# Modulation blocks in bursts of eight and four, with borrowed weight buffers, on one Trainium2 core

## The chip, the core and the metric

The kernel runs on one core of one Trainium2 chip. The time is device microseconds (us) of one execution; three runs of the kernel before gave a median of 3060.91 us. TensorE (PE) multiplies, VectorE (DVE) and ScalarE (ACT) work on its results, SyncE (SP) issues the weight transfers.

## The reference

One layer of a decoder, float32 throughout, for 256 prompt tokens and 8 sequences of 4 sample tokens (T = 288 columns), D = 4096:

```
mod = silu(c) @ w_ada + b_ada  -> shift, scale, gate        # 9 rows of c, w_ada 4096 x 12288
h   = x * (1 + scale) + shift                               # 288 x 4096
[q|k|v|z_a|u|v_b|z_b|g_a|g_b] = h @ w_in                    # 4096 x 18944
A = sliding_window_attention(q, k, v, sinks) * silu(z_a)
B = u * (W_s @ LN(v_b) + b_s) * silu(z_b)
m = sigmoid(g_a) * (A @ w_pa) + sigmoid(g_b) * (B @ w_pb)
x = LayerNorm(ALPHA * x + gate * (m @ w_o))
```

`h` needs all of c's products for its own columns, so the first matmul with `w_in` has to wait for a part of `mod`.

## The kernel before

**Layout.** Features lie on partitions, tokens on the free axis: a *column tile* is 128 output features x 288 tokens, a *k tile* (kt) 128 of the 4096 input features (32 of them). Each weight is read once, in units of 128 x 2048 numbers (1 MB), each by one transfer of SP into a tile `raw` (five buffers, `RAW`). Where the unit is for a main product, ACT rounds it to `wH` (float32r) and DVE takes the rest `wL = raw - wH`, 128 x 1024 at a time (lines 182 and 183). A product of one 128 x 128 block is then three matmuls with 288 columns, `wH*xH`, `wH*xL`, `wL*xH` (`prod`, lines 194 to 196). Sums stand in three PSUM buffers (`acc`); DVE or ACT takes each finished one out.

**Modulation.** The shift and scale columns of w_ada are cut into *chunks* of k tiles, `CHUNKS = [1, 2, 2, 2, 1, 4, 4, 8, 8]`; a chunk of n has 4n blocks of 1 MB (`ada_units`). These are not split: a block is 4 float32 matmuls with 32 stationary columns and 512 moving ones (8 of 256 or 16 of 128 in small chunks), line 234, in four column strips of the array. In the trace each of them stands as two records, in the program as one. After a chunk's last block `fin` lets DVE copy the sums out (`adae`), and a background generator `modulate` has PE transpose them (`adaT`) and DVE and ACT form, k tile by k tile, `xs = x*scale + shift`, `hH` and `hL` (lines 286 to 299).

**Early units.** 56 of the 148 column tiles of `w_in` (part of g_a, k, v, q) are computed chunk by chunk as `h` grows: 113 units in all, `early_units`, tile `ea`. For each column tile and chunk, `early_post` adds the PSUM sum to an accumulator in SBUF (`Q`, `accA`, `accB`, `xs`, lines 340 to 356). A unit of a chunk of n has 16/n column tiles, so 3n matmuls lie between two such sums. The rest of `w_in` (`rest_units`, tile `in`) runs later with 16 k tiles per sum; of 32 of these (zb and u) the half that needs only the first 16 k tiles may run earlier (`extra`).

**What sets the order.** `first_order` writes the order of modulation blocks and early units by a running credit: in the first half (16 k tiles) blocks and early units alternate at a ratio of 1.6 in groups of about two, in the second half two blocks and two other units. It keeps two early units of a chunk (one of the first) back until the next chunk's blocks are through. `run` issues each unit's transfer and split two units ahead. `pump`, called before each product, runs background generators against a credit of 100 for each product; `ensure_h` runs them at once if a unit needs an `h` not yet made. The tile framework then orders instructions within each engine, and each engine executes its own in that order. SP's transfers wait for a free `raw` and for one of eight semaphores that they share with ACT's.

Eight large SBUF buffers (`slot`, 128 x 4608) hold in this stage xs, hH0, hH1, hL0, hL1 (the rounded `h` and its rest, 16 k tiles each), Q, accA and accB.

Of the kernel before, what the change touches and what calls it, by code (L numbers as in the profile page):

```python
# [10 lines left out]
F32 = mybir.dt.float32  # L11
F32R = mybir.dt.float32r
# [6 lines left out]
P = 128  # L19
# [13 lines left out]
TB = 96  # L33
UNIT = 2048

CHUNKS = [1, 2, 2, 2, 1, 4, 4, 8, 8]
RAW = 5
HB = 3
RES = 2
RES0 = 1  # L40
HSTEP = 1
RATIO2 = 1.0
XT = tuple('zb,u'.split(','))
RATIO = 1.6
GE2 = 2.0
GE = 2.0
CAP = 1.5

OFFS = [sum(CHUNKS[:i]) for i in range(len(CHUNKS))]
CQ, CK, CV, CZA, CU, CVB, CZB, CGA, CGB = 0, 16, 18, 20, 36, 52, 68, 84, 116  # L50
# [24 lines left out]
def first_order(au, eu, extra):  # L75

    order = []
    ada = [(c, u) for c, us in enumerate(au) for u in us]  # L80
    early = [(c, u) for c, us in enumerate(eu) for u in us]
    extra = list(extra)
    credit, at, go = 0.0, -1, False
    half = OFFS.index(KT // 2)
    while ada:
        at = ada[0][0]
        ratio = RATIO if at < half else RATIO2
        ready = early and early[0][0] < at
        if ready and at < half and early[0][0] == at - 1 and sum(1 for x in early if x[0] == at - 1) <= (RES if at > 1 else RES0):
            ready = False  # L90
        if credit < 1.0:
            go = False
        elif credit >= (GE if at < half else GE2):
            go = True
        if go and ready:
            order.append(early.pop(0)[1])
            credit -= 1.0
        elif go and at >= half and extra:
            order.append(extra.pop(0))
            credit -= 1.0  # L100
        else:
            order.append(ada.pop(0)[1])
            credit = min(credit + 1.0 / ratio, CAP + 1.0 / ratio + (GE if at < half else GE2) - 1.0)
    return order, extra[:4] + [u for _, u in early] + extra[4:]


def bc(ap, axis, shape):
    return ap.unsqueeze(axis).to_broadcast(list(shape))


def build(ctx, tc, nc, I, O):
    sb = lambda name, bufs=1: ctx.enter_context(tc.tile_pool(name=name, bufs=bufs))
    const, slots, wp, tmp = sb("const"), sb("slots", 8), sb("wp", 4), sb("tmp", 2)
# [6 lines left out]
    def slot(name, shape=(P, 16, T), dt=F32):  # L120
        return slots.tile(list(shape), dt, tag="s", name=name)
# [4 lines left out]
    def bgp(name):  # L126
        return ps_bg.tile([P, 512], F32, tag="bg", name=name)
# [12 lines left out]
    nc.scalar.dma_start(lngb, I["lngb"])  # L140
    nc.vector.memset(epst, EPS)

    hH = [slot(f"hH{i}", dt=F32R) for i in range(2)]
    hL = [slot(f"hL{i}", dt=F32R) for i in range(2)]
    pdram = dram.tile([len(REST), P, T], F32, name="pdram")
    gdram = dram.tile([64, P, T], F32, name="gdram")

# [3 lines left out]
    credit = [0.0]  # L151
# [15 lines left out]
    class Unit:  # L167
        def __init__(self, src, body, split=True, blocks=16):
            self.src, self.body, self.split, self.blocks = src, body, split, blocks

        def start(self):
            raw = wp.tile([P, UNIT], F32, tag="raw", name="raw", bufs=RAW)
            w = self.blocks * P
            nc.sync.dma_start(raw[:, :w], self.src[:, :w])
            self.raw = raw
            self.H, self.L = [], []
            if self.split:
                for hf in range(w // 1024):
                    s = raw[:, hf * 1024:(hf + 1) * 1024]
                    h = wp.tile([P, 1024], F32R, tag="wH", name="wH", bufs=HB)  # L180
                    lo = wp.tile([P, 1024], F32R, tag="wL", name="wL", bufs=HB)
                    nc.scalar.copy(h, s)  # L182
                    nc.vector.tensor_sub(lo, s, h.bitcast(F32))  # L183
                    self.H.append(h)
                    self.L.append(lo)
# [60 lines left out]
    def ada_copies(ps, w):  # L246
        out = []
        for a in range(0, w, 256):
            e = tmp.tile([P, T], F32, tag="t", name="adae", bufs=6)
            nc.vector.tensor_copy(e[:, :min(w - a, 256)], ps[:, a:min(w, a + 256)])  # L250
            out += [e[:, b:b + P] for b in range(0, min(w - a, 256), P)]
        return out

    def ada_transposed(blocks):
        tp = bgp("adaT")
        for i, e in enumerate(blocks):
            nc.tensor.transpose(tp[:, i * P:(i + 1) * P], e, ident)
        return tp[:, :len(blocks) * P].rearrange("p (tb q b) -> p q tb b", q=4, b=32)
# [9 lines left out]
    def load_x(c):  # L268
        n, o = CHUNKS[c], OFFS[c]
        nc.scalar.dma_start(xs[:, 0, :n], I["xT"][:, o:o + n])  # L270

    def ada_fin(c):
        n, o = CHUNKS[c], OFFS[c]

        def modulate(blocks):
            mod = tmp.tile([P, 2, 8, 9], F32, tag="mod", name="mod", bufs=2)
            tpv = ada_transposed(blocks)
            if n < 8:
                b1 = bada[:, :64].rearrange("p (s k) -> p s k", s=2)[:, :, o:o + n]
                nc.vector.tensor_tensor(mod[:, :, :n], tpv[:, 0:2, :, 0:9], bc(b1, 3, (P, 2, n, 9)), ALU.add)  # L280
                nc.vector.tensor_tensor(mod[:, :, :n], mod[:, :, :n], tpv[:, 2:4, :, 0:9], ALU.add)
            else:
                for s in range(2):
                    out = mod[:, s].rearrange("p (q tb) b -> p q tb b", q=2)
                    b1 = bada[:, 32 * s + o:32 * s + o + n].rearrange("p (q tb) -> p q tb", q=2)
                    nc.vector.tensor_tensor(out, tpv[:, 2 * s:2 * s + 2, :, 0:9], bc(b1, 3, (P, 2, 4, 9)), ALU.add)
            nc.vector.tensor_scalar_add(mod[:, 1, :n], mod[:, 1, :n], 1.0)
            for k in range(0, n, HSTEP):
                w = min(HSTEP, n - k)
                x = xs[:, 0, k:k + w]  # L290
                for i in range(w):
                    nc.vector.tensor_scalar(x[:, i, :NPR], x[:, i, :NPR], mod[:, 1, k + i, 0:1], mod[:, 0, k + i, 0:1],
                                            ALU.mult, ALU.add)
                xv = x[:, :, NPR:].rearrange("p n (b t) -> p n b t", t=TS)
                nc.vector.tensor_tensor(xv, xv, bc(mod[:, 1, k:k + w, 1:9], 3, (P, w, NB, TS)), ALU.mult)
                nc.vector.tensor_tensor(xv, xv, bc(mod[:, 0, k:k + w, 1:9], 3, (P, w, NB, TS)), ALU.add)
                a, b = (o + k) // 16, (o + k) % 16
                nc.scalar.copy(hH[a][:, b:b + w], x)  # L298
                nc.vector.tensor_sub(hL[a][:, b:b + w], x, hH[a][:, b:b + w].bitcast(F32))  # L299
            if c + 1 < len(CHUNKS):  # L300
                load_x(c + 1)
            h_done.add(c)
            yield 300

        def fin(ps):
            bg.insert(0, modulate(ada_copies(ps, P * n if n < 8 else 512)))
        return fin

    def gate_fin(gc):
        def finish(blocks):  # L310
            tpv = ada_transposed(blocks)
            out = gate[:, 16 * gc:16 * gc + 16].rearrange("p (q tb) b -> p q tb b", q=4)
            b1 = bada[:, 64 + 16 * gc:80 + 16 * gc].rearrange("p (q tb) -> p q tb", q=4)
            nc.vector.tensor_tensor(out, tpv[:, :, :, 0:9], bc(b1, 3, (P, 4, 4, 9)), ALU.add)
            yield 300

        def fin(ps):
            bg.insert(0, finish(ada_copies(ps, 512)))
        return fin
# [16 lines left out]
    def early_post(e, ps, c):  # L336
        ct, d = EARLY[e], early_dst(e)
        if c == 0:
            if e % 2:
                nc.scalar.copy(d, ps)  # L340
            else:
                nc.vector.tensor_copy(d, ps)
        elif c < len(CHUNKS) - 1:
            nc.vector.tensor_add(d, d, ps)
# [21 lines left out]
    def early_units(c):  # L366
        n, o = CHUNKS[c], OFFS[c]
        per = 16 // n
# [532 lines left out]
    items = []  # L901
# [17 lines left out]
    au = [ada_units(n, ada_fin(c)) for c, n in enumerate(CHUNKS)]  # L919
    gu = [u for gc in range(GATE_CHUNKS) for u in ada_units(8, gate_fin(gc))]  # L920
    eu = [early_units(c) for c in range(len(CHUNKS))]
    extra = [ru[r][0] for r, (k, _) in enumerate(REST) if k in XT]
    order, rest = first_order(au, eu, extra)
    items += order
    ru = [us[1:] if k in XT else us for us, (k, _) in zip(ru, REST)]
    n_vb = sum(k == "vb" for k, _ in REST)
    body = rest + flat(ru[:first_vb]) + [drain] + flat(ru[first_vb:first_vb + 2 * n_vb]) + [drain]
# [4 lines left out]
    order = [pu[0][0], pu[1][0], pu[0][1]]  # L932
# [96 lines left out]
```

## Time and profile before

| what | value |
|---|---|
| runs | 3060.25, 3060.91, 3063.03 us |
| the profiled execution | 3059.19 us, of which the span of the program is 3057.4 us |
| PE busy | 3017.8 us of the span |
| DVE, ACT busy | 1571.4 us, 1077.9 us |
| PE idle before 24 us / from 24 to 600 us / from 600 to 1000 us | 15.5 / 12.7 / 0 us |
| bytes read from memory | 676.85 MB |

Modulation and early units fill the stretch from 0 to about 823 us of the span. In the profile, times stand in us from the start of the span; `[2.00 <-ACT wH L182]` behind a row is idle time of that engine before it, and what ended it. A PE that is busy all the time can still be slow: a matmul is shown for some 0.29 us while the next starts 0.13 us after it, so what counts is the step from one start to the next.

### The profile page before, as it was taken

How to read it: one execution, taken by the hardware profiler on the slowest of the kernel's cores; microseconds unless marked ns; L12 is line 12 of the kernel's file. 1: busy time of each engine (PE TensorE's matmuls, PEld its weight loads, DVE VectorE, ACT ScalarE, POOL GpSimd, SP SyncE). 2: the span in 40 equal slices, each digit the busy share in tenths (PEclk: the TensorE clock that was granted, in tenths of full speed). 3: DMA queues.
4: the chain of work that ended last, by engine and by line, in shares of the span. 5: the costliest groups of instructions: out<-in, count | busy, mean ns of one | idle time of the engine just before them, and what ended most of it. 6: DMA issues, size and time to landing. Idle time of an engine off the chain costs nothing.

```text
span 3057.4 us, 53584 instructions
## 1 busy us (share of the span) xinstructions
PE 3017.8 (99%) x23168; PEld 2844.2 (93%) x23168; DVE 1571.4 (51%) x2262; ACT 1077.9 (35%) x1381; POOL 17.5 (1%) x16
## 2 busy tenths in 40 slices
PE   7999999999999999999999999999999999999998
PEld 6887888888999999999999999999999999999997
DVE  4777554444445545454444643445555555555555
ACT  3222322322332434344333333333444444433333
POOL 0000000000000000000000000000000000000001
PEclk9999999999999999999999999999999999999998
DMA  8888877877767565565655565666565555555552
GB/s 328 334 321 323 340 281 285 318 262 286 276 235 249 198 221 211 209 219 191 217 193 207 207 216 215 222 226 222 196 218 187 187 188 189 175 177 177 177 177 96
DMA packets 128672, 700.09 MB, mean 229 GB/s; under 512 B 14834, under 2 KB 44818, under 8 KB 49298
## 3 DMA queue, kind: packets, MB, share of 16 engines
q1 hardware_dynamic: 109584, 669.56, 60.6%
q10 hardware_dynamic: 18852, 27.10, 2.5%
q8 instruction: 182, 2.98, 0.4%
q14 instruction: 54, 0.44, 0.0%
HBM read 676.85 MB, written 19.46 MB: 228 GB/s over the span
## 4 chain that ended last, share of the span: by engine, by line
PE 97%; DVE 1%; DMA 1%; issue 0%; ACT 0%; DVEq 0%; SPq 0%; ACTq 0%
PE in L194 13%; PE in L196 13%; PE in L195 13%; PE ea L194 8%; PE ea L196 8%; PE ea L195 8%; PE ada L234 5%; PE p L194 5%; PE y L194 5%; PE y L196 4%; PE p L196 4%; PE y L195 4%; PE p L195 4%; DMA raw<-we 1%; DVE wL L183 0%
## 5 line engine op out<-in xcount | busy, mean ns | idle before, releaser
L183 DVE TENSOR_TENSOR wL<-raw,wH 128x1024 fp32r<-128x1024 f32 x848 | 1034.0, 1224 | 991.2 <-ACT wH L182 990.6
L182 ACT CAST wH<-raw 128x1024 fp32r<-128x1024 f32 x848 | 885.0, 1048 | 1857.1 <-PE in L195 666.8
L194 PE MATMUL in<-hH,wH 128*128 128x288 f32 x2944 | 879.4, 299 | 0.0
L195 PE MATMUL in<-hL,wH 128*128 128x288 f32 x2944 | 869.9, 295 | 0.0
L196 PE MATMUL in<-hH,wL 128*128 128x288 f32 x2944 | 866.1, 294 | 0.0
L194 PEld LDWEIGHTS in<-hH,wH 128*128 128x128 f32 x2944 | 552.0, 187 | 21.8 <-issue 13.9
L196 PEld LDWEIGHTS in<-hH,wL 128*128 128x128 f32 x2944 | 554.5, 188 | 0.8 <-DVE wL L183 0.8
L195 PEld LDWEIGHTS in<-hL,wH 128*128 128x128 f32 x2944 | 553.0, 188 | 0.2
L194 PE MATMUL ea<-hH,wH 128*128 128x288 f32 x1792 | 538.3, 301 | 10.8 <-ACT hH L298 5.2
L195 PE MATMUL ea<-hL,wH 128*128 128x288 f32 x1792 | 529.5, 296 | 1.7 <-DVE hL L299 1.7
L196 PE MATMUL ea<-hH,wL 128*128 128x288 f32 x1792 | 525.8, 295 | 1.4 <-DVE wL L183 1.4
L194 PEld LDWEIGHTS ea<-hH,wH 128*128 128x128 f32 x1792 | 336.5, 188 | 53.1 <-ACT wH L182 24.7
L196 PEld LDWEIGHTS ea<-hH,wL 128*128 128x128 f32 x1792 | 337.6, 189 | 3.0 <-DVE wL L183 2.1
L195 PEld LDWEIGHTS ea<-hL,wH 128*128 128x128 f32 x1792 | 337.9, 189 | 2.4 <-DVE hL L299 2.2
L194 PE MATMUL y<-mH,wH 128*128 128x288 f32 x1024 | 303.2, 296 | 0.0
L195 PE MATMUL y<-mL,wH 128*128 128x288 f32 x1024 | 302.4, 295 | 0.0
L196 PE MATMUL y<-mH,wL 128*128 128x288 f32 x1024 | 301.1, 294 | 0.0
L234 PE MATMUL ada<-raw,cT 128*32 128x512 f32 (+2 forms) x1920 | 193.7, 518 | 10.3 <-ACT cT L137 8.3
L196 PEld LDWEIGHTS y<-mH,wL 128*128 128x128 f32 x1024 | 192.9, 188 | 0.1
L195 PEld LDWEIGHTS y<-mL,wH 128*128 128x128 f32 x1024 | 192.3, 188 | 0.1
L194 PEld LDWEIGHTS y<-mH,wH 128*128 128x128 f32 x1024 | 191.9, 187 | 0.0
L194 PE MATMUL p<-AH,wH 128*128 128x288 f32 x512 | 151.8, 296 | 0.0
(202 smaller groups left out, 2410.1 us busy)
## 6 DMA issues: line engine op xcount, KB each, us to landing
raw<-wada SPq DMA_DIRECT2D x192, 1024.0 KB, 5.1
raw<-wr SPq DMA_DIRECT2D x184, 1024.0 KB, 6.2
raw<-we SPq DMA_DIRECT2D x111, 1024.0 KB, 7.6
raw<-wo SPq DMA_DIRECT2D x64, 1024.0 KB, 4.9
raw<-wpa SPq DMA_DIRECT2D x32, 1024.0 KB, 4.8
raw<-wpb SPq DMA_DIRECT2D x32, 1024.0 KB, 4.9
gl<-gdram SPq DMA_DIRECT2D x64, 144.0 KB, 3.3
pdram<-part ACTq DMA_DIRECT2D x32, 144.0 KB, 4.9
```

What stands on the lines that cost most here:

```text
L182: nc.scalar.copy(h, s)
L183: nc.vector.tensor_sub(lo, s, h.bitcast(F32))
L194: mm(ps, wh, xh, start=first, stop=False)
L195: mm(ps, wh, xl, start=False, stop=False)
L196: mm(ps, wl, xh, start=False, stop=last)
L234: mm(st["ps"][32 * q:32 * q + 32, :w], cT[:, kt, :], u.raw[:, at:at + w], start=kt < 1 + paired, stop=kt >= KT - 1 - paired)
```

## The change

The chunks become 1, 1, 2, 4, 4, 4, 8, 8. The order is written out directly: in the first half the blocks of a chunk go in bursts of up to eight, with the previous chunk's early units spread between the bursts and the last one or two of these kept for after the chunk's last burst; in the second half four blocks, then four other units (early ones as long as more than two are left, then extras). Two large buffers that later hold hH1 and hL1 serve until then as four more `raw` buffers (`room`), so nine transfers can be held in the first half; in the second there are five again. Both generators first yield 400, so the transposes are put about four products later. hH1 and hL1 are made only when chunk 6 writes them. There are still 128 blocks for shift and scale and 113 early units.

```diff
-CHUNKS = [1, 2, 2, 2, 1, 4, 4, 8, 8]
+CHUNKS = [1, 1, 2, 4, 4, 4, 8, 8]
 RAW = 5
...
+BORROWED = 4
+BURST = 8
+BURST2 = 4
...
-    while ada:
-        at = ada[0][0]
-        ratio = RATIO if at < half else RATIO2
...
+    first, left = list(au[0]), []
+    for c in range(1, half):
+        mine = list(eu[c - 1])
+        keep = [mine.pop(2)] if len(mine) == 4 else [mine.pop() for _ in range(2)][::-1]
+        bursts = [au[c][i:i + BURST] for i in range(0, len(au[c]), BURST)]
+        first += left
+        for i, x in enumerate(bursts):
+            first += mine[len(mine) * i // len(bursts):len(mine) * (i + 1) // len(bursts)] + x
+        left = keep
+    second, early, extra = [], left + list(eu[half - 1]), list(extra)
+    for c in range(half, len(CHUNKS)):
+        for i in range(0, len(au[c]), BURST2):
+            take = min(BURST2, max(0, len(early) - 2))
+            second += early[:take] + extra[:BURST2 - take] + au[c][i:i + BURST2]
+            early, extra = early[take:], extra[BURST2 - take:]
+        early = early + list(eu[c])
+    return first, second, extra[:4] + early + extra[4:]
...
-    hH = [slot(f"hH{i}", dt=F32R) for i in range(2)]
-    hL = [slot(f"hL{i}", dt=F32R) for i in range(2)]
+    hH, hL = [slot("hH0", dt=F32R)], [slot("hL0", dt=F32R)]
+
+    room = [slot(f"room{i}", (P, 4608)) for i in range(BORROWED // 2)]
+    room = [r[:, i * UNIT:(i + 1) * UNIT] for r in room for i in range(2)]
...
         def start(self):
-            raw = wp.tile([P, UNIT], F32, tag="raw", name="raw", bufs=RAW)
+            at = taken[0] % (RAW + BORROWED)
+            taken[0] += 1
+            if self.early and at >= RAW:
+                raw = room[at - RAW]
+            else:
+                raw = wp.tile([P, UNIT], F32, tag="raw", name="raw", bufs=RAW)
...
         def modulate(blocks):
+            yield 400
...
+                if a == len(hH):
+                    hH.append(slot(f"hH{a}", dt=F32R))
+                    hL.append(slot(f"hL{a}", dt=F32R))
...
         def finish(blocks):
+            yield 400
```

How the instructions stand now, at three places. The line numbers of the changed kernel are a little lower in the matmuls and the split (233 for the modulation matmuls, 193 to 195 for the products, 182 for `wL`) and higher in the adds of `early_post` (348 for 344).

**PE, a run of modulation blocks in the first half** (chunks of 4: a block is four matmuls of 512). Before, within a chunk of 4:

```order
L195 MATMUL ea<-hL_92,wH 128x288
L196 MATMUL ea<-hH_90,wL 128x288
L194 MATMUL ea<-hH_90,wH 128x288
L195 MATMUL ea<-hL_92,wH 128x288
L196 MATMUL ea<-hH_90,wL 128x288
L234 MATMUL ada<-raw,cT 32x512 x12
L194 MATMUL ea<-hH_90,wH 128x288
L195 MATMUL ea<-hL_92,wH 128x288
```

and now, the first burst of chunk 4:

```order
L193 MATMUL ea<-hH_90,wH 128x288
L194 MATMUL ea<-hL_91,wH 128x288
L195 MATMUL ea<-hH_90,wL 128x288
L233 MATMUL ada<-room_93,cT 32x512 x4
L233 MATMUL ada<-raw,cT 32x512 x20
L233 MATMUL ada<-room_92,cT 32x512 x8
L193 MATMUL ea<-hH_90,wH 128x288
L194 MATMUL ea<-hL_91,wH 128x288
```

A run of three blocks has become one of eight, out of nine buffers. Over PE's whole list, runs of modulation matmuls up to the last block for shift and scale go from 72 to 42 (with the gate's later ones from 90 to 60).

**PE, where the first chunk of 8 is through.** Before (chunk 7):

```order
L234 MATMUL ada<-raw,cT 32x512 x4
L257 MATMUL adaT<-ident,adae 128x128 x2
L234 MATMUL ada<-raw,cT 32x512 x4
L257 MATMUL adaT<-ident,adae 128x128 x2
L234 MATMUL ada<-raw,cT 32x512 x8
L194 MATMUL ea<-hH_91,wH 128x288 x3
L195 MATMUL ea<-hL_93,wH 128x288
```

and now (chunk 6, the same k tiles):

```order
L233 MATMUL ada<-raw,cT 32x512 x16
L193 MATMUL ea<-hH_90,wH 128x288
L194 MATMUL ea<-hL_91,wH 128x288
L195 MATMUL ea<-hH_90,wL 128x288
L193 MATMUL ea<-hH_90,wH 128x288
L194 MATMUL ea<-hL_91,wH 128x288
L256 MATMUL adaT<-ident,adae 128x128 x2
L195 MATMUL ea<-hH_90,wL 128x288
L256 MATMUL adaT<-ident,adae 128x128 x2
L193 MATMUL ea<-hH_90,wH 128x288
L194 MATMUL ea<-hL_91,wH 128x288
```

The transposes now stand five matmuls into an early unit of chunk 5 (12 matmuls for each sum, read from hH0), where before they stood among modulation blocks and the next matmul was one of the new `h` (hH_91).

**DVE, the end of that chunk's modulation.** Before, the chunk's last rows and the first adds behind them:

```order
L296 TENSOR_TENSOR xs<-xs,mod 128x32
L295 TENSOR_TENSOR xs<-xs,mod 128x32
L296 TENSOR_TENSOR xs<-xs,mod 128x32
L299 TENSOR_TENSOR hL_93<-xs,hH_91 128x288 x2
L344 TENSOR_TENSOR accB<-accB,ea 128x288 x3
```

and now:

```order
L302 TENSOR_TENSOR hL_5871<-xs,hH_5870 128x288
L292 TENSOR_SCALAR xs<-xs,mod 128x256
L302 TENSOR_TENSOR hL_5871<-xs,hH_5870 128x288
L295 TENSOR_TENSOR xs<-xs,mod 128x32
L348 TENSOR_TENSOR Q<-Q,ea 128x288
L296 TENSOR_TENSOR xs<-xs,mod 128x32
L348 TENSOR_TENSOR Q<-Q,ea 128x288 x2
L302 TENSOR_TENSOR hL_5871<-xs,hH_5870 128x288
```

Before, no sum of PE's was due while this chain ran, since its users follow it. Now the first `Q<-Q,ea` belongs to the early unit that covers the chain, and it stands behind all but two of the chain's rows and behind two `wL` splits that lie among them. In chunk 3 (4 k tiles, covered by units of chunk 2 with 6 matmuls for each sum) the first such add stands likewise behind most of the chain and three splits; in chunk 4 it stands second in the chain, and in chunk 5 right behind the chain's head and two splits, with two more splits further on.

More of the change, by code (lines that the diff above doesn't have):

```diff
@@ L34 @@
 UNIT = 2048
-CHUNKS = [1, 2, 2, 2, 1, 4, 4, 8, 8]
+CHUNKS = [1, 1, 2, 4, 4, 4, 8, 8]
 RAW = 5
 HB = 3
-RES = 2
-RES0 = 1
+BORROWED = 4
+BURST = 8
+BURST2 = 4
 HSTEP = 1
-RATIO2 = 1.0
 XT = tuple('zb,u'.split(','))
[L44 to L47, printed above, removed]
 OFFS = [sum(CHUNKS[:i]) for i in range(len(CHUNKS))]
@@ L75, in first_order @@
 def first_order(au, eu, extra):
[L79 to L83, printed above, removed]
-    half = OFFS.index(KT // 2)
-    while ada:
-        at = ada[0][0]
-        ratio = RATIO if at < half else RATIO2
[L88 to L104, printed above, removed]
+    half = OFFS.index(KT // 2)
+    first, left = list(au[0]), []
[15 more added lines that the diff above has]
+    return first, second, extra[:4] + early + extra[4:]
 def bc(ap, axis, shape):
@@ L141, in build @@
     nc.vector.memset(epst, EPS)
-    hH = [slot(f"hH{i}", dt=F32R) for i in range(2)]
-    hL = [slot(f"hL{i}", dt=F32R) for i in range(2)]
+    hH, hL = [slot("hH0", dt=F32R)], [slot("hL0", dt=F32R)]
+    room = [slot(f"room{i}", (P, 4608)) for i in range(BORROWED // 2)]
+    room = [r[:, i * UNIT:(i + 1) * UNIT] for r in room for i in range(2)]
+    taken = [0]
     pdram = dram.tile([len(REST), P, T], F32, name="pdram")
@@ L169, in __init__ @@
             self.src, self.body, self.split, self.blocks = src, body, split, blocks
+            self.early = False
         def start(self):
-            raw = wp.tile([P, UNIT], F32, tag="raw", name="raw", bufs=RAW)
+            at = taken[0] % (RAW + BORROWED)
[4 more added lines that the diff above has]
+                raw = wp.tile([P, UNIT], F32, tag="raw", name="raw", bufs=RAW)
             w = self.blocks * P
@@ L922, in build @@
     extra = [ru[r][0] for r, (k, _) in enumerate(REST) if k in XT]
-    order, rest = first_order(au, eu, extra)
-    items += order
+    first, second, rest = first_order(au, eu, extra)
+    for u in first:
+        u.early = True
+    items += first + second
     ru = [us[1:] if k in XT else us for us, (k, _) in zip(ru, REST)]
```

## Prediction

> **What bounds the kernel now.** I read the page's busy times, its slices and its chain first, then PE's idle time by stage, then what ended it.
>
> ```profile
> span 3057.4 us, 53584 instructions
> PE 3017.8 (99%) x23168; PEld 2844.2 (93%) x23168; DVE 1571.4 (51%) x2262; ACT 1077.9 (35%) x1381; POOL 17.5 (1%) x16
> PEclk9999999999999999999999999999999999999998
> PE 97%; DVE 1%; DMA 1%; issue 0%; ACT 0%; DVEq 0%; SPq 0%; ACTq 0%
> ```
>
> PE is the bound nearly throughout, and 97% of the chain that ended last is PE. So the change can gain in two ways alone: fewer PE idle gaps, or PE work that takes fewer steps. The gaps by stage (PE's busy time is the second number, taken from the window's length):
>
> ```profile
> 0.00:24.00 24.00, 8.51 (x135) 6.68 (x136) 5.23 (x12) 5.71 (x6) 0.20 (x4) 0.92 0.93 376
> 24.00:600.00 576.00, 563.34 (x4423) 482.36 (x4423) 348.33 (x630) 166.94 (x202) 0.00 (x0) 0.99 0.82 314
> 600.00:1000.00 400.00, 400.00 (x3017) 371.55 (x3016) 192.21 (x266) 123.17 (x129) 0.00 (x0) 1.00 0.74 266
> ```
>
> Up to 24 us PE idles 15.5 us on the first transfers and the first chunk. That head has the same transfers and the same chunk of 1 after the change, so I leave it. From 24 to 600 us it idles 12.7 us, and after that not at all until the tail. Who ended those 12.7 us, by PE's groups in that window:
>
> ```profile
> L194 PE MATMUL ea<-hH,wH 128*128 128x288 f32 x923 | 279.4, 304 | 5.9 <-ACT wH L182 2.0 <-DVE accB L344 1.6 <-DVE Q L344 0.9
> L195 PE MATMUL ea<-hL,wH 128*128 128x288 f32 x924 | 273.1, 297 | 1.3 <-DVE hL L299 1.3
> L196 PE MATMUL ea<-hH,wL 128*128 128x288 f32 x923 | 270.3, 296 | 1.4 <-DVE wL L183 1.4
> L257 PE MATMUL adaT<-ident,adae 128*128 128x128 f32 x19 | 4.2, 299 | 3.5 <-DVE adae L250 3.5
> ```
>
> No gap there was ended by a transfer. All come from DVE and ACT around the making of `h`: the copies before the transposes, the new `h`, splits, and adds that free PSUM. So what the change is worth hangs on the switches that bursts save and on the gaps around `h`, and not on the nine buffers as such.
>
> **The switch between products and modulation.** Two runs of modulation blocks, one of two blocks and one of four:
>
> ```profile
> 415.87 0.29 PE L196 MATMUL ea<-hH,wL 128*128 128x288 f32 x1
> 416.09 1.93 PE L234 MATMUL ada<-raw,cT 128*32 128x512 f32 x16
> 417.94 0.40 PE L194 MATMUL ea<-hH,wH 128*128 128x288 f32 x1
> 418.18 0.29 PE L195 MATMUL ea<-hL,wH 128*128 128x288 f32 x1
> ...
> 306.00 0.29 PE L196 MATMUL ea<-hH,wL 128*128 128x288 f32 x1
> 306.23 3.64 PE L234 MATMUL ada<-raw,cT 128*32 128x512 f32 x32
> 309.80 0.40 PE L194 MATMUL ea<-hH,wH 128*128 128x288 f32 x1
> 310.04 0.30 PE L195 MATMUL ea<-hL,wH 128*128 128x288 f32 x1
> ```
>
> Products start 0.13 us apart. From the last product ahead of a run to the second behind it are 2.31 us for two blocks and 4.04 us for four. Less two ordinary steps (0.27) that is 2.04 and 3.77. So a block costs 0.86 us and a run 0.31 to 0.33 us beside its blocks: PE is slow to go into the strips, out of them, and on its first product after (0.24 for 0.13). None of it shows as idle time. The runs go from 72 to 42. 30 x 0.33 gives -9.9 us. Bounds: -8 us, if a quarter of the removed runs were cut out where PE waits anyway, and -10.5 us.
>
> **The gaps around `h`.** Here the change adds. Each early unit's sum must be added by DVE before its PSUM buffer, one of three, is free. DVE's rows of the first chunk of 8, the split and the add:
>
> ```profile
> 593.55 0.46 DVE L344 TENSOR_TENSOR accB<-accB,ea 128x288 f32<-128x288 f32 x1 [0.21 <-PE ea L196]
> 596.57 3.49 DVE L183 TENSOR_TENSOR wL<-raw,wH 128x1024 fp32r<-128x1024 f32 x3
> ...
> 583.92 0.37 DVE L286 TENSOR_TENSOR mod<-adaT,bada 128x72 f32<-128x72 f32 x2 [1.57 <-PE adaT L257]
> 590.82 0.18 DVE L295 TENSOR_TENSOR xs<-xs,mod 128x32 f32<-128x32 f32 x1
> 591.40 0.83 DVE L299 TENSOR_TENSOR hL<-xs,hH 128x288 fp32r<-128x288 f32 x2 [0.17 <-ACT hH L298]
> ```
>
> Eight k tiles take DVE from 583.92 to 592.2, 8.3 us. Chunk 6 in the changed kernel: PE starts an early unit of chunk 5, five matmuls later come the transposes, and until all three PSUM buffers are used 31 matmuls are left, 31 x 0.133 = 4.1 us. DVE needs some 0.4 us to start, does the chain up to its eighth L295 (583.92 to 591.0, 7.1 us, and one hL more, 0.4), two splits (2 x 1.16) and the first add (0.5): 10.7 us. PE idles 10.7 - 4.1 = 6.6 us, and I take 6.4 us. Before, this place held 1.57 us of the L257 row and 0.28 us.
> Chunk 2: two k tiles behind a unit of chunk 1 with three matmuls for each sum. Before, chunk 1 stood just so behind chunk 0:
>
> ```profile
> 53.54 0.44 PE L257 MATMUL adaT<-ident,adae 128*128 128x128 f32 x2 [0.55 <-DVE adae L250]
> 55.98 0.40 PE L194 MATMUL ea<-hH,wH 128*128 128x288 f32 x1 [2.00 <-ACT wH L182]
> 57.24 0.79 PE L196 MATMUL ea<-hH,wL 128*128 128x288 f32 x3 [0.21 <-DVE wL L183]
> 58.27 0.61 PE L194 MATMUL ea<-hH,wH 128*128 128x288 f32 x1 [0.25 <-ACT Q L340]
> 63.27 0.40 PE L195 MATMUL ea<-hL,wH 128*128 128x288 f32 x1 [1.27 <-DVE hL L299]
> ```
>
> These are 4.3 us; chunk 2 has the same, with adds in place of plain copies, so 4.8. Chunks 1 and 4 and what else is short: 2.4 us. Chunk 7 is covered by extras with 48 matmuls for each sum, which ACT takes out: nothing.
> Chunk 3, four k tiles behind units of chunk 2: the transposes stand right behind the burst (0.6 us for the copy, like the first of these rows), the chain is half as long (4.2) with three splits (3.5), and three sums of six matmuls cover 2.4 us. 0.6 + 7.7 - 2.4 is 5.9; a little runs after the first add, so 5.4.
> Chunk 5: the adds are spread through the chain, with five splits. It lies between 0.6 us (a copy alone) and 8.8 - 4.8 = 4 us (4.2 + 4 x 1.16 against three sums of 12 matmuls); I take 3.2, nearer the computed end.
> The sum is 6.4 + 5.4 + 3.2 + 4.8 + 2.4 = 22.2 us for the 12.7 that go: +9.5 us. Bounds: +2, if chunks 3 and 5 get by with a copy's wait (0.6 each), and +14, if a second pause of the size of chunk 5's follows in each of chunks 3 and 4.
>
> **The granted clock.** The last three numbers of a window are the clock, the transfers' share and GB/s:
>
> ```profile
> 20.00:40.00 20.00, 17.95 (x118) 15.24 (x118) 13.42 (x24) 11.17 (x22) 0.00 (x0) 0.83 0.67 267
> 40.00:60.00 20.00, 17.00 (x177) 12.96 (x177) 9.02 (x23) 6.82 (x13) 0.00 (x0) 0.94 0.97 373
> 60.00:80.00 20.00, 18.58 (x159) 16.50 (x158) 16.27 (x27) 6.91 (x11) 0.00 (x0) 0.97 0.70 261
> 100.00:120.00 20.00, 18.72 (x155) 16.26 (x154) 15.43 (x35) 6.96 (x8) 0.00 (x0) 1.00 0.95 386
> ```
>
> After the head's gaps the clock lacks 0.17 x 20 = 3.4 us; after the gaps at 53 to 58 us, 0.06 x 20 + 0.03 x 20 = 1.8 us. The second goes with its place. The changed kernel has three places of that kind or longer (chunks 2, 3, 6), so up to 3 x 1.8 - 1.8 = 3.6 us more. Most of it falls while PE waits for DVE anyway: I take +1.0, with bounds 0 and 3.6.
> [...]
>
> **Other parts.** The counts of blocks (128) and early units (113) stay, so no matmul or byte goes. Eight chunks in place of nine save one set of transposes and 56 adds of 128 x 288 on DVE. These cost 0.46 us each (the L344 row above), some 26 us, but DVE is 51% busy: I take nothing on PE. Moved transfers: SP may now hold nine blocks. A burst of eight drains 8 x 0.86 = 7 us of PE time. Until the next burst PE has six units of 48 matmuls, 6 x 6.4 us, so 45 us for 14 blocks or 14.7 MB: 327 GB/s. Two of the 20 us windows above reach 373 and 386 GB/s. So I cost the transfers at nothing; their cover is the six units, and without it each late block would cost 1.05 MB / 380 GB/s = 2.8 us. hH1 and hL1 wait for the last reader of the borrowed room, which has read it before the second half starts: nothing. The late transposes hide the copy that PE now waits for at some chunks (3.5 us in the L257 row above), but in chunks 2, 3 and 5 the program still has them right behind the last block.
>
> **The sum.** 3059.2 (the profiled execution) - 9.9 + 9.5 + 1.0 = 3059.8. That execution lies 1.7 us below the median of the runs, so the forecast is 3061.5 us, no change. A measurement of this kernel can tell about 0.2%, 6.1 us, from no change.
>
> **Rivals.**
> First, the burst gain comes alone: DVE's adds come through between the chain's steps as before, and the gaps stay near 12.7 us. Then 3060.9 - 9.9 = 3051 us. For it speaks that 12.7 us held nine chunks and eight remain; against it, the order has the adds behind the chains of chunks 3 and 6. Chance 0.13.
> Second, slower by the clock: each of the pauses of chunks 3 and 6 costs as much clock as the head's, 3.4 us, and chunk 2's 1.8. That is 8.6 - 1.8 = 6.8 us in place of 1.0: 3067.3 us, and with the pauses at their upper bound (+14) 3072 us. It decides where more than about 6 us of clock and pauses come on top of my sum. For it speaks the 0.83 in the window after the head; against it, that PE waits for DVE in the same stretch. Chance 0.16.
> Third, transfers become the bound: bursts of eight leave the buffers empty and the next splits late, some three blocks of 2.8 us each, 3070 us. For it speaks that the second window runs at a share of 0.97; against it the 327 GB/s needed on the average. Chance 0.06.
> My forecast has 0.65. Its own range is 3056 to 3066; with the rivals on both sides, 3053 to 3069 leaves about 0.2 out. Faster by over 0.2% gets 0.14, within it 0.66, slower 0.20.
>
> **What would show it.** Right: runs of eight and four blocks in PE's rows with the same 0.33 us beside each; no PE idle ended by a transfer after 24 us; PE idle of 19 to 25 us between 24 us and the end of the second half's blocks, with one pause of 5 to 7 us near 610 us ended by a DVE add of `Q`, and clusters near 80 and 145 us; a granted clock under 1 at those places. Wrong: a pause near 610 us under 3 us (first rival), or `raw` as releaser of PE or of ACT's splits with PE idle behind it (third).

## The result, and the profile after

The changed kernel takes 3068.78 us (median of 9 runs, 3065.84 to 3071.96), the kernel before beside it 3060.91 us (9 runs): a ratio of 1.0026, with a 95% interval of 1.0018 to 1.0035. It is 7.9 us slower, a little over the 6.1 us that a measurement can tell. The forecast was 3061.5 us and no change, with a chance of 0.20 for slower; the time is 7.3 us above the forecast. It lies inside the range of 3053 to 3069 by 0.2 us, and four of the nine runs lie above it: that it is inside is luck.

The page of the changed kernel: span and instructions, busy times, and the shares of the chain that ended last.

```profile
span 3064.6 us, 53260 instructions
PE 3012.6 (98%) x23040; PEld 2848.5 (93%) x23040; DVE 1543.2 (50%) x2203; ACT 1077.1 (35%) x1381; POOL 17.5 (1%) x16
PE 96%; DVE 2%; DMA 1%; issue 0%; ACT 0%; DVEq 0%; SPq 0%; ACTq 0%
```

PE is busy 5.2 us less than before (3012.6 for 3017.8), and the span is 7.2 us longer: the change did save PE work, and lost more in pauses. Where, by stage (PE's busy time is the second number; the granted clock, the transfers' share and GB/s are the last three):

```profile
0.00:24.00 24.00, 8.75 (x136) 6.90 (x137) 5.28 (x12) 5.71 (x6) 0.20 (x4) 0.86 0.93 371
24.00:600.00 576.00, 560.09 (x4297) 490.82 (x4297) 312.67 (x525) 167.54 (x201) 0.00 (x0) 0.99 0.78 304
600.00:1000.00 400.00, 392.64 (x2971) 364.42 (x2971) 192.66 (x281) 123.75 (x136) 0.00 (x0) 0.99 0.72 269
80.00:100.00 20.00, 15.62 (x112) 11.29 (x111) 14.97 (x35) 2.96 (x4) 0.00 (x0) 0.83 0.96 387
150.00:170.00 20.00, 16.28 (x103) 15.70 (x102) 17.69 (x41) 6.43 (x9) 0.00 (x0) 0.83 1.02 423
610.00:630.00 20.00, 12.64 (x83) 12.41 (x82) 14.78 (x45) 7.44 (x12) 0.00 (x0) 0.83 0.82 327
```

Between 24 and 1000 us PE idles 15.9 + 7.4 = 23.3 us, for 12.7 before. In three short windows the granted clock is 0.83: 3.4 of 20 us are missing in each. Before, only the place at 53 to 61 us lost clock after the head. What ended PE's pauses between 24 and 1000 us (time, count, longest), and the one wait of that kind between 1400 and 1600 us:

```profile
PE ea L193 <- DVE Q L348: 9.7, 4, 7.4
PE ea L195 <- DVE wL L182: 4.1, 2, 2.6
PE adaT L256 <- DVE adae L249: 3.0, 4, 1.4
PE ea L193 <- DVE accB L348: 2.3, 2, 1.5
...
PE ada L233 <- DMA raw<-wada: 1.8, 1, 1.8
```

The 7.4 us are the pause at chunk 6, read here on PE and then on DVE:

```profile
613.34 0.29 PE L195 MATMUL ea<-hH,wL 128*128 128x288 f32 x1
620.99 0.61 PE L193 MATMUL ea<-hH,wH 128*128 128x288 f32 x1 [7.36 <-DVE Q L348]
621.39 0.44 PE L194 MATMUL ea<-hL,wH 128*128 128x288 f32 x1
621.63 0.44 PE L195 MATMUL ea<-hH,wL 128*128 128x288 f32 x1
```

```profile
609.68 0.37 DVE L286 TENSOR_TENSOR mod<-adaT,bada 128x72 f32<-128x72 f32 x2 [0.65 <-PE adaT L256]
...
612.76 1.23 DVE L182 TENSOR_TENSOR wL<-raw,wH 128x1024 fp32r<-128x1024 f32 x1 [1.07 <-ACT wH L181]
...
620.38 0.18 DVE L295 TENSOR_TENSOR xs<-xs,mod 128x32 f32<-128x32 f32 x1
620.49 0.45 DVE L348 TENSOR_TENSOR Q<-Q,ea 128x288 f32<-128x288 f32 x1
```

PE fills its three PSUM buffers and stops. DVE does all but the last two rows of the chain of eight k tiles, with two splits among them, before the first add of an early sum. Behind the pause products start 0.24 us apart, not 0.133: the clock is at half (granted 0.50 from 617.96 to 624.78 us).

### The profile page after: what moved, and what is told of

It is laid out like the page before. It is cut to its first block, busy times and chain, and to the rows that moved or that the text cites. A ratio compares the mean times of both kernels' runs of the same rounds, so it can differ in the third digit from the quotient of the medians.

```text
span 3064.6 us, 53260 instructions
## 1 busy us (share of the span) xinstructions
PE 3012.6 (98%) x23040; PEld 2848.5 (93%) x23040; DVE 1543.2 (50%) x2203; ACT 1077.1 (35%) x1381; POOL 17.5 (1%) x16
## 4 chain that ended last, share of the span: by engine, by line
PE 96%; DVE 2%; DMA 1%; issue 0%; ACT 0%; DVEq 0%; SPq 0%; ACTq 0%
PE in L193 13%; PE in L195 13%; PE in L194 13%; PE ea L193 8%; PE ea L194 7%; PE ea L195 7%; PE ada L233 6%; PE p L193 5%; PE y L193 5%; PE y L195 4%; PE p L195 4%; PE y L194 4%; PE p L194 4%; DMA raw<-we 1%; DVE wL L182 1%
## 5 line engine op out<-in xcount | busy, mean ns | idle before, releaser
L182 DVE TENSOR_TENSOR wL<-raw,wH 128x1024 fp32r<-128x1024 f32 x812 | 989.5, 1224 | 1036.0 <-ACT wH L181 1030.2
L181 ACT CAST wH<-raw 128x1024 fp32r<-128x1024 f32 x812 | 845.7, 1048 | 1749.9 <-PE in L194 594.7
L233 PE MATMUL ada<-raw,cT 128*32 128x512 f32 (+2 forms) x1512 | 159.4, 552 | 11.6 <-ACT cT L127 8.4
```

The costliest lines, as they stand in the source:

```text
L233: mm(st["ps"][32 * q:32 * q + 32, :w], cT[:, kt, :], u.raw[:, at:at + w], start=kt < 1 + paired, stop=kt >= KT - 1 - paired)
```

## The experiments

Differences between kernels are differences of medians; the ratio to the kernel before has its interval. For reference:

| kernel | us | to before | interval |
|---|---|---|---|
| changed, again | 3068.88 | 1.0027 | 1.0017 to 1.0038 |
| fill_pause | 3064.95 | 1.0014 | 1.0006 to 1.0023 |
| cover_c6 | 3058.45 | 0.9993 | 0.9984 to 1.0002 |
| cover_pairs | 3054.68 | 0.9979 | 0.9970 to 0.9988 |
| chunks_alone | 3069.83 | 1.0029 | 1.0019 to 1.0040 |
| no_room | 3117.20 | 1.0183 | 1.0164 to 1.0201 |
| old_list | 3062.85 | 1.0006 | 0.9997 to 1.0015 |
| two_two | 3047.36 | 0.9952 | 0.9938 to 0.9965 |
| two_two_threes | 3043.19 | 0.9941 | 0.9928 to 0.9953 |
| two_two_eights | 3046.74 | 0.9959 | 0.9946 to 0.9973 |
| second_pairs | 3048.04 | 0.9958 | 0.9945 to 0.9970 |
| two_two_no_room | 3050.55 | 0.9968 | 0.9956 to 0.9980 |

**The changed kernel again.**

> The changed kernel once more, so that the next three stand beside it on one chip. Every theory expects the result again: 6 to 9 us over the kernel before (0.2 to 0.3%), a pause of about 7 us near 620 us and half clock there for 6 to 7 us. If the pauses near 88, 153 and 620 us carry the loss, the clock is lost at the same three places; if the places of lost clock wander from execution to execution, they are not caused by the pauses.

It came out at 3068.88 us, with a pause of 7.22 us at chunk 6. The clock was at half at the same three places, but for 3.41, 3.41 and 6.83 us, where the first profiled execution had 6.83 us at each. So the places are the pauses'; how long the half clock lasts changes from execution to execution.

**Is the clock lost because PE pauses?** The pause of chunk 6 is filled with products that nobody reads:

```diff
             tpv = ada_transposed(blocks)
+            if o == KT // 2:
+                fill = bgp("fill")
+                for i in range(50):
+                    mm(fill[:, :T], hH[0][:, 0, :P], hH[0][:, 0], start=True, stop=True)
             if n < 8:
```

> The changed kernel with 50 more products of 128 x 288 into a spare PSUM buffer, put on PE right behind the four transposes of chunk 6 (nothing reads them; nothing else is moved). They take 50 x 0.133 = 6.7 us and lie where PE now idles 7.36 us, since the early products that stand behind them wait for DVE's adds anyway. PE gets 6.7 us more work and keeps busy. Theory one, the clock follows the pause: the pause shrinks to about 1 us, no clock is lost near 620 us, and the time is some 3.4 us below the changed kernel's (half clock for 6.8 us is worth 3.4 us) in spite of the added work; 3 to 4 us slower than before. Theory two, the clock is lost for another reason, or its loss falls into time in which PE waits anyway: the time stays at the changed kernel's, 7 to 8 us slower than before. Theory three, the pause is not a wait for DVE: the products come on top, 6 to 7 us over the changed kernel.

PE's group of these products between 600 and 640 us, and the window that had a clock of 0.83:

```profile
L281 PE MATMUL fill<-hH 128*128 128x288 f32 x50 | 7.1, 297 | 0.0
610.00:630.00 20.00, 20.00 (x155) 20.00 (x152) 16.06 (x48) 7.57 (x13) 0.00 (x0) 1.00 0.89 358
```

With 50 products more, the kernel is 3.9 us faster than without them. PE has no pause there, the clock is full, and the other two places keep their half clock (6.83 us each). Theory one holds, and shows that the pause causes the loss of clock. Its size needs care: from chunk 6's transposes to chunk 7's the trace has 244.66 us in the changed kernel and 241.95 here, 2.7 us less. Of 6.83 us at half clock 3.0 fell in the pause itself; the slow steps behind it cost 1.8 us, and 0.7 us of pause went as well. The rest of the 3.9 us is within what two medians can differ by.

**What is the whole pause worth?** Chunk 6's chain gets other work in front of it:

```diff
-            take = min(BURST2, max(0, len(early) - 2))
+            take = 0 if c > half and i < BURST2 else min(BURST2, max(0, len(early) - 2))
```

> The changed kernel with one number altered: the first group of chunk 7 has four extra units ahead of its burst (48 matmuls for each sum, which ACT takes out) and no early units, so that chunk 6's chain on DVE is covered by work that needs no DVE add. Runs and transfers stay. Theory one, pause and clock of chunk 6 are a loss of their own: the pause near 620 us (7.4) and the half clock there (3.4) both go, 10 to 11 us below the changed kernel, so 2 to 4 us faster than before. Theory two, the loss comes back later, because the four early units move behind and the extras are then missing elsewhere: within 3 us of the changed kernel. Theory three, only the pause counts, the clock does not: 7 us below the changed kernel, equal to before.

```profile
610.00:630.00 20.00, 20.00 (x153) 20.00 (x152) 15.12 (x42) 10.02 (x17) 0.00 (x0) 1.00 1.01 408
```

This is the same window: no idle time, full clock. The time is 10.4 us below the changed kernel's: theory one, pause and clock both. From transposes to transposes it is 236.15 us for 244.66, 8.5 us less: 7.4 of pause, 1.8 of slow steps (the expectation had 3.4), less a new pause of 0.56 us at 646 us. The profiled execution, the slowest of the eleven (3062.37 us), then gave 3.4 us back up to the gate's first transposes, most of it in a pause of 0.73 us at 950 us and in a stretch at half clock at 1516 us (granted 0.91 from 1512 to 1532 us); so the medians rest on the other executions. One pause, which the prediction had in its place and within 1 us of its size, is enough to make the loss: without it the kernel stands 2.7 us below before, which can't be told from no change.

**Are bursts of eight worth having?** The same kernel with `BURST = 2`:

> The same with bursts of two blocks in place of eight in the first half (the second half keeps its groups of four). PE has 14 more runs of modulation blocks than in the kernel with the covered chunk 6. Theory one, a run costs 0.33 us and nothing else changes: 14 x 0.33 = 4.6 us slower than that kernel. Theory two, the bursts bring gaps of their own around the new h (adds of several early units queued behind a chain, transposes right behind the last block), so that pairs lose 4.6 us in runs and get it back in shorter pauses and less half clock near 88 and 153 us: within 2 us of it.

The expectation counted runs on the five own buffers alone. With those on borrowed buffers the program has 84 runs, not 60: 24 more, 7.9 us at 0.33 us. And yet it is 3.8 us faster, and the times of the two kernels do not overlap (3051.79 to 3055.99 us for 3057.32 to 3062.37). From 24 to 600 us, first with bursts of eight, then in pairs:

```profile
24.00:600.00 576.00, 559.60 (x4290) 490.25 (x4289) 313.11 (x525) 167.43 (x201) 0.00 (x0) 0.98 0.77 303
...
24.00:600.00 576.00, 568.63 (x4330) 491.16 (x4332) 316.92 (x527) 170.99 (x205) 0.00 (x0) 0.99 0.79 305
```

PE idles 16.4 us with bursts and 7.4 in pairs. Theory two: in the first half the long bursts lost in pauses and clock more than they saved in runs.

**The list of chunks alone**, put into the kernel before:

```diff
-CHUNKS = [1, 2, 2, 2, 1, 4, 4, 8, 8]
+CHUNKS = [1, 1, 2, 4, 4, 4, 8, 8]
```

> The kernel before with the changed kernel's list of chunks alone (1,1,2,4,4,4,8,8 for 1,2,2,2,1,4,4,8,8); its order of blocks by credits, its five buffers and its hH and hL stay. Theory one, the list itself costs: with fewer and larger chunks each chain of DVE is longer and the early units behind it are fewer, so the pauses near 88 and 153 us come without any burst, and five buffers may also run dry: 5 us or more slower than before. Theory two, the list is harmless (one set of transposes and 56 adds on DVE less) and the pauses near 88 and 153 us belong to the bursts: within 3 us of before.

It is 9.1 us slower than before. PE's longest waits from 24 to 600 us, and the window at 150 us:

```profile
PE ada L234 <- DMA raw<-wada: 4.4, 5, 1.4
PE ea L196 <- DVE wL L183: 3.8, 2, 2.4
PE ea L194 <- DVE accB L344: 2.4, 1, 2.4
...
150.00:170.00 20.00, 14.84 (x59) 8.72 (x60) 10.41 (x29) 5.71 (x8) 0.00 (x0) 0.53 1.01 422
```

Theory one: the pauses near 88 us belong to the list, not to the bursts, and with five buffers the first chunk of four runs out of blocks, while the transfers are at a share of 1.01. Four of the five waits for `raw`, 4.1 of the 4.4 us, lie there, and half clock for 20.5 us goes with them.

**The borrowed room.** The changed kernel without it (`if False and self.early and at >= RAW:`):

> The changed kernel with the five raw buffers alone; the order of bursts and units stays, the four borrowed buffers are not used. Theory one, the six units ahead of a burst cover its transfers only because nine blocks can be held: with five, three or four blocks of each burst come at the rate of the transfers, and each 1 MB block lands 2.45 us after the one ahead of it (the rate of the packets at 8 to 24 us) where PE needs 0.86 us: some 1.6 us x 3 or 4 for each of about eight bursts, 35 to 55 us slower than the changed kernel, with raw as PE's releaser. Theory two, five buffers are enough, as before: within 3 us of the changed kernel.

It is 48 us slower than the changed kernel. Two of PE's waits from 24 to 600 us:

```profile
PE ada L233 <- DMA raw<-wada: 22.0, 17, 3.1
...
PE ea L193 <- ACT wH L181: 6.4, 5, 2.1
```

Theory one, by the transfers that are named. They are not all of the 48 us: from 24 to 600 us PE idles 45.0 us for the changed kernel's 15.9, and the granted clock is 0.94 there for 0.99. For a burst of eight, the room is what keeps the prediction's zero for the transfers true.

**The list of before with the rest**, that is cover_pairs with `CHUNKS = [1, 2, 2, 2, 1, 4, 4, 8, 8]`:

> The kernel with the covered chunk 6 and bursts of two, with the list of before, 1,2,2,2,1,4,4,8,8. Theory one, the list 1,1,2,4,4,4,8,8 is no gain in itself: nine chunks with their smaller chains do as well or better than its eight (which have the pauses at 87 and 154 us), within 3 us of the kernel with pairs. Theory two, each chunk more costs transposes, sums and a chain of its own: 5 us or more slower than the kernel with pairs, about the time of before.

8.2 us slower than cover_pairs: theory two. Eight chunks are better than nine, once their pauses are small.

**One chunk less**, cover_pairs with `CHUNKS = [2, 2, 4, 4, 4, 8, 8]`:

> The kernel with the covered chunk 6 and bursts of two in the first half, and the list of chunks 2,2,4,4,4,8,8: one chunk less, and no chunk of two k tiles behind a chunk of one with its three matmuls for each sum. Theory one, the pauses at 83 to 87 us go with their place, and one set of sums less has 40 products fewer to start: PE idles some 3 us more in the head, where the first chunk now needs two k tiles' blocks; on balance 2 to 6 us below the kernel with pairs, some 3050 us. Theory two, the longer head costs as much as the pauses do, since PE has nothing else to do there: within 2 us of that kernel, or slower.

It gains 7.3 us more, but not by theory one alone. The transposes of the first chunk of four, eight k tiles into the work in both, first in cover_pairs, then here:

```profile
144.52 0.44 PE L256 MATMUL adaT<-ident,adae 128*128 128x128 f32 x2 [0.55 <-DVE adae L249]
...
137.92 0.44 PE L256 MATMUL adaT<-ident,adae 128*128 128x128 f32 x2 [0.55 <-DVE adae L249]
```

6.6 us are won by then, though PE idles no less up to 140 us (19.2 us for 17.5, from its busy times of 120.78 and 122.47 us). The win is PE work: 66 runs for 84, and fewer of the lone pieces told of at the end. The "40 products fewer" of the expectation were wrong: no product goes, the matmuls that go are modulation's, 832 for 896 in the program. That by itself wins nothing: in the trace of before a run of four blocks takes 3.78 us in 32 matmuls of 256 columns (at 135.05 us) and 3.77 us in half as many of 512 (at 306.23 us; from the last product ahead to the second behind, less two steps).

**Threes, eights and the second half.** The kernel of two_two with `BURST = 3`:

> The same with bursts of three in the first half. Theory one, runs of 0.33 us and gaps trade evenly between two and four blocks: within 2 us of the kernel with pairs. Theory two, runs of three lie so that the adds come through between the bursts, and save two runs and the pauses behind chunk 3 and 4: 3 us or more below it.

with `BURST = 8`:

> The kernel with the chunks 2,2,4,4,4,8,8 and the covered chunk 6 with bursts of eight in the first half, as in the changed kernel; PE has 42 runs of modulation blocks in all, for 60 with bursts of three and 66 with pairs, and each burst stands whole (in the changed kernel chunk 2's were cut into pieces). Theory one, with whole bursts and one chunk less the saved runs decide: 18 runs fewer than with threes at 0.24 to 0.33 us, 4 to 6 us below 3043 us. Theory two, a burst of eight costs more in pauses around the new h (adds of six units behind one chain, splits late) and in half clock behind them than its runs save, on this list too: 3046 to 3052 us, with pauses and half clock back near 140, 250 and 360 us.

and with threes and `BURST2 = 2` (the extras ahead of chunk 7 as they were):

> The kernel with the chunks 2,2,4,4,4,8,8, bursts of three in the first half and the covered chunk 6, with groups of two blocks in place of four in the second half (BURST2 = 2; the first two groups of chunk 7 keep their four extras). PE has 16 more runs of modulation blocks, all in a stretch where it does not idle. Theory one, a run costs 0.33 us beside its blocks (read from two runs of the profile before): 16 x 0.33 = 5.3 us slower than with groups of four, PE busy throughout. Theory two, a run's price is part of the blocks' own and the grouping is free: within 2 us. Theory three, smaller groups let DVE and the transfers through more evenly and win back more than the runs cost: faster.

The threes have the best time of all, 3043.19 us, 17.5 us below before beside it (ratio 0.9941) and 25.6 below the changed kernel. The window of 24 to 600 us with threes, then with eights:

```profile
24.00:600.00 576.00, 566.39 (x4318) 496.82 (x4311) 302.51 (x491) 175.06 (x211) 0.00 (x0) 0.98 0.80 310
...
24.00:600.00 576.00, 559.43 (x4293) 495.91 (x4286) 299.43 (x488) 173.16 (x209) 0.00 (x0) 0.98 0.78 308
```

Eights save 18 runs and PE idles 7.0 us more (16.6 for 9.6). Their 3046.74 us is against theory one, which had them 4 to 6 us below the threes; that eights are slower than threes can't be told, the intervals overlap. In the second half, where PE does not idle, 16 runs more cost 4.8 us by the medians, again with overlapping intervals. The traces are finer. Chunk 5's and chunk 7's transposes with threes, then with second_pairs:

```profile
357.01 0.38 PE L256 MATMUL adaT<-ident,adae 128*128 128x128 f32 x2
830.05 0.38 PE L256 MATMUL adaT<-ident,adae 128*128 128x128 f32 x2
...
355.05 0.38 PE L256 MATMUL adaT<-ident,adae 128*128 128x128 f32 x2
831.23 0.38 PE L256 MATMUL adaT<-ident,adae 128*128 128x128 f32 x2
```

476.18 us for 473.04: 3.1 us, and 1.4 us of pauses at 452, 570 and 630 us that went, for 16 runs: 0.28 us a run. Theory one, a little below its price; the rows of the runs themselves, 2.05 us for two blocks and 3.77 for four, give it in full (2 x 2.05 - 3.77 = 0.33).

**Pairs without the room** (two_two, five buffers for all):

> The kernel with the chunks 2,2,4,4,4,8,8, bursts of two and the covered chunk 6, without the borrowed buffers: five raw buffers for everything. Theory one, the room is needed for long bursts alone: in pairs five buffers do nearly as well, within 8 us of the same kernel with the room (some waits of 1 to 3 us near 105 to 120 us, where blocks and units of the small chunks both want the transfers). Theory two, the room is worth as much as without it in the kernel with bursts of eight: 40 to 50 us slower.

3.2 us slower than two_two by the medians, with overlapping intervals, and so within theory one's 8 us. The room is worth 48 us to bursts of eight and at most a few us to pairs.

## Why the prediction was right or wrong, step by step

**The runs: right.** A run of eight blocks after the change, ahead of it and behind it two products:

```profile
207.59 0.29 PE L195 MATMUL ea<-hH,wL 128*128 128x288 f32 x1
207.81 1.06 PE L233 MATMUL ada<-room,cT 128*32 128x512 f32 x8
208.69 4.48 PE L233 MATMUL ada<-raw,cT 128*32 128x512 f32 x40
212.99 1.90 PE L233 MATMUL ada<-room,cT 128*32 128x512 f32 x16
214.82 0.40 PE L193 MATMUL ea<-hH,wH 128*128 128x288 f32 x1
215.05 0.30 PE L194 MATMUL ea<-hL,wH 128*128 128x288 f32 x1
```

7.46 us less two steps (0.27) and eight blocks of 0.86 us is 0.31 us, as for two and four blocks. Over all PE steps from start to start, the changed kernel spends 11.8 us less in modulation and on the products beside a run; -9.9 was forecast. The 30 runs are 9.9 us of it at 0.33 us. Most of the rest, some 1.7 us, is that fewer blocks are cut elsewhere than at whole sets of four matmuls; this is an estimate, from the sets of four in both traces, begun ones counted whole, at the price of the rows at the end of this document. The working's "no matmul or byte goes" is wrong for matmuls: modulation has 896 in the program for 960 before, since one chunk of four takes the place of two of two. That alone is worth nothing: four blocks took 3.78 us in matmuls of 256 columns, 3.77 in half as many of 512.

**The pauses around h: right in their places, near in their sizes.** +9.5 us was forecast and +10.6 found; the misses of the places, 1.0 and 1.6 us up and 1.1 and 0.4 us down, cancel in part:

| place | forecast | found |
|---|---|---|
| chunk 6 | 6.4 | 7.4 |
| chunk 3 | 5.4 | 4.3 |
| chunk 2 | 4.8 | 4.4 |
| chunk 5 | 3.2 | 3.2 |
| rest | 2.4 | 4.0 |

Chunk 6's extra 1.0 us has its row above: within the chain DVE waits 1.07 us for ACT to round the next unit, which the working left out.

**The granted clock: the term that was mis-sized.** +1.0 us was forecast, with 3.6 as the upper bound. Counted over the product steps at half rate, the three places cost 2.2, 2.3 and 1.8 us, 6.3 together, for the 1.4 us of the place at 58 us before: +4.9. In the second profiled execution they cost 4.2 us: +2.8. The step that failed is "most of it falls while PE waits for DVE anyway". Of 6.83 us at half rate at each place, PE's pauses hid 3.0 at chunk 6, but 1.8 at chunk 2 and 1.2 at chunk 3. And the bound took its 1.8 us a place from one that was at half clock for 3.41 us; in the first profiled execution each of the three was so for twice as long.

**The transfers: costed at nothing, and 1.8 us found.** No wait for a transfer appeared between 24 and 1000 us. The one at 1520 us is a modulation block of the gate, long after the bursts, in a stretch that the prediction did not look at. Every kernel here with the new `first_order` has it (1.2 to 2.4 us), before and chunks_alone don't. What in the order makes that block late was not tried. By the letter the prediction's sign "no PE idle ended by a transfer after 24 us" was not met.

So -11.8 + 10.6 + 4.9 + 1.8 = +5.5 us, of the 7.2 us between the two spans; 1.7 us stay unassigned. Put together from the forecast, the 5.5 us are its own 0.6, the misses of the clock (3.9), the transfer (1.8) and the pauses (1.1), less the 1.9 us that the runs saved beyond their term. The profiled execution lies 2.4 us below its median, before's 1.7 below.

**The rivals.** The second, slower by the clock, named these three places and gave 3067.3 to 3072 us; the time is in it, though the clock came to 4.9 us in the first profiled execution and 2.8 in the second, not to its 6.8. "It decides where more than about 6 us of clock and pauses come on top" was met by clock, pauses and a transfer together. The first fell at the pause near 610 us. The third did not come with nine buffers; with five it would have, at 3117 us.

## What to carry to other kernels

Price a longer burst by what stands behind it, not by the switches alone: 30 runs of 0.33 us were real, and one pause that the reorder opened, 7.4 us and its clock, gave them back. Where a chain of small operations on DVE must finish before sums are added, put work ahead of it whose sums another engine takes out; one changed line did so for 10.4 us. And when bursts lengthen, buffers for them are a condition: without the room the same order lost 48 us.

## What the runs showed of the hardware

**Where the clock fell.** In the traces of before and of the changed kernel, every stretch at one rate between the first change and the last is a whole number of 3.413 us: 3.41, 6.83 or 10.24 us at half clock, and at full clock in the changed kernel 61.44, 58.03, 457.39 and 2413.22 us (18, 17, 134 and 707 of them). Cut into steps of that length at the changes, the two traces have, from 20 to 3000 us, four steps at full clock in which PE idles more than 1.60 us. Half clock followed each:

| kernel | step, us | PE idle in it, us | half clock behind it, us |
|---|---|---|---|
| before | 54.20 to 57.61 | 1.99 | 3.41 |
| changed | 85.48 to 88.89 | 2.05 | 6.83 |
| changed | 150.33 to 153.75 | 2.55 | 6.83 |
| changed | 614.55 to 617.96 | 3.41 | 6.83 |

The next three, 1.60 us (before, 579.85 us), 1.44 and 1.43 us (changed, 1519.08 and 375.61 us), were followed by full clock. So it is not the length of one pause: at 88 us 1.51 and part of 1.46 us lay in one step, and the pause of 1.84 us at 1520 us, with 1.44 of it in one step, cost no clock (granted 1.00 from 1512 to 1532 us). No one limit holds for all places: in the head of the changed kernel a step with 1.63 us (13.80 us) was followed by half clock, and in its tail, where PE runs matmuls of one column that are each shown as busy for some 0.3 us, one with 1.15 us of shown idle time (3034.60 us). The changes lie 3.00 us past a multiple of 3.413 us from the start of the span in before and 0.15 us in the changed kernel, so the two executions cut a cluster of pauses at different places. The least that stands behind a step of the table is 3.41 us at half clock, 1.7 us of clock before what the pauses hide: the 1.8 us a place that the prediction took for its upper bound is about the least seen.

**A lone piece cost as much as four.** In the changed kernel chunk 2's bursts are cut into pieces on PE, such as this one of a single matmul (two records):

```profile
60.38 0.29 PE L195 MATMUL ea<-hH,wL 128*128 128x288 f32 x1
60.60 0.62 PE L233 MATMUL ada<-room,cT 128*32 128x256 f32 x2
61.15 0.40 PE L193 MATMUL ea<-hH,wH 128*128 128x288 f32 x1
61.39 0.30 PE L194 MATMUL ea<-hL,wH 128*128 128x288 f32 x1
```

From product to second product it takes 1.01 us, 0.74 more than two steps; a run of eleven such matmuls at 63.75 us takes 1.62. A run of two at 78.04 us takes 0.75 and one of four at 55.89 us 0.77, hardly more than the lone one; one of six at 57.87 us takes 1.18. Less 0.33 us for the run, the lone matmul costs 0.41 us, the four together 0.44, and each of the eleven 0.12. In these rows four matmuls, one for each column strip, took about the time of one, so a run of this kernel is best cut at whole sets of four. The prediction counted such pieces as runs like any other. In PE's order cover_pairs has 12 single matmuls and two_two 5.
